# A hybrid decoder block: the short convolution's first gate joins the product stage, the state-space scan runs in three runs a block, the next head's jobs come first, the product stage's tiles are placed anew

## The chip, the core and the metric

The kernel runs on one core of a Trainium2 chip. Times are device microseconds (us) of that core. The engines are TensorE (PE in the profile; its weight loads are PEld), VectorE (DVE), ScalarE (ACT), GpSimd (POOL) and SyncE (SP, which here issues transfers).

## The reference

One layer over 16 meta tokens and 1024 tokens of width 1024. A normalised stream goes through one wide input projection, three mixers read parts of it, each mixer's output is projected, weighted by a sigmoid gate and merged, and one more projection follows.

```python
xn = rms_norm(x, norm_pre)
proj = xn @ w_in                                  # 1024 x 13856
(ssd_z, ssd_xbc, ssd_dt, sc_b, sc_c, sc_h, sc_g,
 dn_qkv, dn_z, dn_b, dn_a, gate_logits) = jnp.split(proj, ...)
y_ssd = ssd_mixer(...)     # conv, scan over chunks of 64, silu(z) gate, grouped rms_norm
y_sc  = short_conv_mixer(...)
y_dn  = gated_deltanet_mixer(...)   # 8 heads of 128: conv, l2 norm, delta rule, rms_norm, silu(z)
branch = jnp.einsum("btnw,nwd->btnd", jnp.stack([y_ssd, y_sc, y_dn], axis=2), w_branch)
merged = jnp.sum(jax.nn.sigmoid(gates) * branch, axis=2)
return x + rms_norm(merged @ w_out, norm_post)

def short_conv_mixer(b_gate, c_gate, h, gate, conv_w):
    y = b_gate * causal_depthwise_conv(c_gate * h, conv_w)
    return y * jax.nn.silu(gate)
```

The short convolution has four column blocks of the projection: c and h (before the convolution), the gate (`sc_g`) and b.

## The kernel before

Feature rows lie on the 128 partitions, tokens along the free axis. The normalised stream is held in the memory beside the engines as two parts, `xh` (the rounded value) and `xl` (the rest), tiles of 128 x 8 x 1040. A weight tile is split in the same way, and each product is three matmuls: xh by w high, xl by w high, xh by w low. They are called dense here; in the mixing stage lines 187 to 189 issue them, in the product stage lines 1144 to 1146.

**The mixing stage** (to 1217.8 us) is a list of jobs. A job is one block of 128 columns of the projection over all tokens: 8 k-tiles x 3 dense matmuls for each of three groups of 342 to 348 tokens, or of two groups of 512 where the meta tokens are not wanted. Each gated-delta head needs four jobs (`dn`+head+k, q, v, z). A tile t of the short convolution has three in this kernel, `sc`+t+c, h and g: `c * h`, its convolution on DVE, then the SiLU of g and the product, which goes to DRAM as `conv`. The state-space branch has jobs B and C for each of two groups, x and z for each of eight tiles.

The jobs fill slots, and each slot is woven with one mixer part: `dn_mix(h)` for the 8 heads (names `dm0` to `dm7`), `sd_mix(t)` for the 8 state-space tiles (`sm0` to `sm7`). The mixer is a generator, and each `yield` names a price that dense work should cover before the next piece of mixing; the table `GAPS` scales these by the kind of the slot. What is written out is the order on each engine, which runs its instructions in that order. Slot h of the heads holds the four jobs of head h+1 and some of the short convolution; the last state-space slot (kind `sl`) has three of the short convolution.

```python
    for h, n in enumerate((3, 3, 2, 3, 2, 3, 2, 3)):
        ...
        slot(4 + n, lambda h=h: beside(lambda: dn_mix(h, dnt[h]), early, 9), lambda n=n: sc_next(n), *fs)
```

The pieces that matter here: `dn_mix` turns k and v to token order (L508), multiplies k by q and k by k (L582, L587), solves the chunk's triangle in small 16-bit products, and runs the scan (L693 to L714: `ks`, `pn`, `su`, `o`); the norm of the head's output comes last (`ms`, L734 and L735). `sd_mix` does the same for the scan of the states (L852 to L876: `o`, `su`, the state `H`, `dg`) and sums squares for the grouped norm, whose reciprocal row (`sqa`, L901) goes to DRAM as `rin_d` (L902).

**The product stage** (from 1217.8 us) multiplies eight groups in a form with seven block products in place of eight (`py` and `pz` are its sums, each four quarters of 12 dense matmuls): the last gate of the short convolution (`cb`), for each branch its merging gate and its projection, and the output projection. The first product of a group whose input is the normalised stream reads `xh` and `xl` in place; other inputs are loaded (`tr`), then split on ACT (L1108) and DVE (L1109) into `th` and `tl`. Weights are split at L1124 and L1125. The state-space output is read back, scaled by `rin_d` (`scale_tasks`) and written out for its projection beside the first groups.

Of the kernel before, what the change touches and what calls it, by code (L numbers as in the profile page):

```python
# [1357 lines left out]
```

## Time and profile before

| | |
|---|---|
| Median of 3 runs | 1842.95 us (1842.75 to 1843.3) |
| Profiled execution, its own time | 1845.19 us |
| Its span, from the first to the last instruction | 1843.2 us |
| Mean granted TensorE clock | 0.996 |
| PE busy | 1806.2 us, 98% |
| DVE, ACT, POOL busy | 1302.7, 860.5, 220.3 us |
| Mixing stage, product stage | 0 to 1217.8, 1217.8 to 1843.2 us |

A busy matmul in the profile is shown with a duration that includes its pipeline, so two neighbours overlap; the spacing of work on PE is read from start to start. Instructions that the profile joins are counted by "x" at the row's end. The text in brackets behind a row is idle time of that engine just before it and what ended it.

### The profile page before, as it was taken

What the parts mean: (1) busy time and instruction counts of PE and PEld (TensorE: products, weight loads), DVE (VectorE), ACT (ScalarE), POOL (GpSimd) and SP (SyncE); (2) the same over time, 40 slices, a digit from 0 to 9 for tenths busy, and PEclk for the clock granted to TensorE, in tenths of its full rate; (3) what the DMA queues carried; (4) which work ended last, traced back from release to release, by engine and by line L of the source; (5) the groups of instructions that cost most, each with busy time, mean ns of one, the idle gap of its engine ahead of it and who ended that gap; (6) DMA issues with size and microseconds to landing.
All of it is one profiled execution on the core that took longest, in us unless ns stands there. A gap on an engine that the chain in (4) does not pass through costs nothing.

```text
span 1843.2 us, 27628 instructions
## 1 busy us (share of the span) xinstructions
PE 1806.2 (98%) x11067; PEld 1564.2 (85%) x11067; DVE 1302.7 (71%) x1898; ACT 860.5 (47%) x1373; POOL 220.3 (12%) x369
## 2 busy tenths in 40 slices
PE   6999999999999999999999999999999999999997
PEld 5988989888888889888989988978888888888886
DVE  6585766757576656757578867886686857967787
ACT  5443435353344425353445555445544455455454
POOL 3011111210112111110111101101000310000000
PEclk9999999999999999999999999999999999999999
DMA  5123262532224131202335323166566898763522
GB/s 156 49 70 104 75 172 61 132 87 90 59 64 114 47 81 39 65 26 62 75 90 175 84 77 104 35 222 228 175 218 230 295 289 222 209 192 133 194 98 92
DMA packets 149259, 229.96 MB, mean 125 GB/s; under 512 B 11393, under 2 KB 89406, under 8 KB 148458
## 3 DMA queue, kind: packets, MB, share of 16 engines
q1 hardware_dynamic: 129170, 166.31, 28.4%
q0 software_dynamic: 15344, 47.19, 10.6%
q10 hardware_dynamic: 4616, 14.69, 2.0%
q8 instruction: 87, 1.43, 0.3%
q14 instruction: 42, 0.34, 0.1%
HBM read 191.36 MB, written 68.27 MB: 141 GB/s over the span
## 4 chain that ended last, share of the span: by engine, by line
PE 85%; issue 4%; DVE 4%; DMA 3%; ACT 2%; POOL 1%; SPq 0%; DVEq 0%; ACTq 0%; POOLq 0%
PE py L1146 5%; PE py L1144 5%; PE py L1145 5%; PE pz L1145 4%; PE pz L1146 4%; PE pz L1144 4%; DMA ys<-y_sd 2%; DVE gt L1231 1%; DMA rin<-rin_d 0%; DMA gain<-in_norm_pre_dram 0%; DVE tl L1109 0%; DVE w L1125 0%; DMA raw<-in_w_in_dram 0%; PE sm L364 0%; PE dn7q L187 0%
## 5 line engine op out<-in xcount | busy, mean ns | idle before, releaser
L1146 PE MATMUL py<-th,w 128*128 128x512 f32 x496 | 193.2, 389 | 1.6 <-DVE w L1122 1.0
L1145 PE MATMUL py<-tl,w 128*128 128x512 f32 x496 | 193.0, 389 | 0.0
L1144 PE MATMUL py<-th,w 128*128 128x512 f32 x496 | 193.0, 389 | 0.0
L1109 DVE TENSOR_TENSOR tl<-tr,th 128x1024 fp32r<-128x1024 f32 x108 | 130.7, 1222 | 66.6 <-ACT th L1108 66.1
L1108 ACT CAST th<-tr 128x1024 fp32r<-128x1024 f32 x108 | 113.0, 1053 | 113.6 <-PE py L1146 53.6
L1144 PE MATMUL pz<-th,w 128*128 128x512 f32 x368 | 143.2, 389 | 0.0
L1145 PE MATMUL pz<-tl,w 128*128 128x512 f32 x368 | 143.2, 389 | 0.0
L1146 PE MATMUL pz<-th,w 128*128 128x512 f32 x368 | 143.2, 389 | 0.0
L1146 PEld LDWEIGHTS py<-th,w 128*128 128x128 f32 x496 | 93.1, 188 | 21.7 <-DVE w L1122 1.4
L1145 PEld LDWEIGHTS py<-tl,w 128*128 128x128 f32 x496 | 93.1, 188 | 19.4
L1144 PEld LDWEIGHTS py<-th,w 128*128 128x128 f32 x496 | 93.1, 188 | 19.3
L166 DVE TENSOR_TENSOR w<-raw,w 128x1024 fp32r<-128x1024 f32 x76 | 92.9, 1223 | 11.6 <-ACT w L165 11.3
L165 ACT CAST w<-raw 128x1024 fp32r<-128x1024 f32 x76 | 79.6, 1047 | 17.0 <-PE sc4h L189 8.3
L1145 PEld LDWEIGHTS pz<-tl,w 128*128 128x128 f32 x368 | 69.1, 188 | 14.4
L1144 PEld LDWEIGHTS pz<-th,w 128*128 128x128 f32 x368 | 69.1, 188 | 14.3
L1146 PEld LDWEIGHTS pz<-th,w 128*128 128x128 f32 x368 | 69.1, 188 | 14.3
L1156 ACT COPY u<-py 128x1024 f32<-128x1024 f32 x34 | 34.5, 1015 | 56.2 <-PE py L1146 56.2
L1169 DVE TENSOR_TENSOR u<-pz,u 128x1024 f32<-128x1024 f32 x34 | 41.3, 1218 | 4.2 <-PE pz L1146 4.2
L1265 POOL COPY tick<-th 128x1 f32<-128x1 f32 x12 | 14.7, 1228 | 120.5 <-ACT th L1108 120.5
L1175 ACT ACTIVATE gt<-u 128x1024 f32<-128x1024 f32 x14 | 14.8, 1059 | 28.9 <-DVE u L1169 25.7
L479 ACT ACT_TABLE_LOAD x20 | 25.7, 1283 | 4.8 <-PE sd2z L189 1.4
L500 ACT ACT_TABLE_LOAD x19 | 24.4, 1283 | 0.3
(1858 smaller groups left out, 5446.8 us busy)
## 6 DMA issues: line engine op xcount, KB each, us to landing
raw<-in_w_in_dram SPq DMA_DIRECT2D x76, 512.0 KB, 4.2
tr<-x_t SPq DMA_DIRECT2D x32, 512.0 KB, 4.2
tr<-x SPq DMA_DIRECT2D x14, 512.0 KB, 6.3
ys<-y_sd POOLq DMA_DIRECT2D x16, 256.0 KB, 7.3
tr<-dn_t SPq DMA_DIRECT2D x8, 512.0 KB, 6.2
gt<-conv SPq DMA_DIRECT2D x4, 1024.0 KB
tr<-sc_t SPq DMA_DIRECT2D x8, 512.0 KB, 3.8
tr<-sd_t SPq DMA_DIRECT2D x8, 512.0 KB, 3.8
```

Source lines behind the costliest of these rows:

```text
L165: A.copy(wh, raws[i])
L166: V.tensor_tensor(wl, raws[i], wh.bitcast(F32), ALU.subtract)
L479: lambda o, c0, n: A.activation(dst[:, c0 - META:c0 - META + n], o, fn), name=name)
L500: A.activation(f, f, AF.Exp)
L1108: A.copy(h, src)
L1109: V.tensor_tensor(l, src, h.bitcast(F32), SUB)
L1144: PE.matmul(o, lhsT=w[:, 0, k, cs], rhs=r1, start=fresh and k == 0, stop=False, skip_group_check=not fresh)
L1145: PE.matmul(o, lhsT=w[:, 0, k, cs], rhs=r2, start=False, stop=False, skip_group_check=not fresh)
L1146: PE.matmul(o, lhsT=w[:, 1, k, cs], rhs=r1, start=False, stop=k == HK - 1, skip_group_check=not fresh)
L1156: A.copy(t, g.ps["y", u])
L1169: V.tensor_tensor(k, t, k, ADD)
L1231: V.scalar_tensor_tensor(o, o, tot, fin["x", t][:, es], ALU.mult, ADD)
```

## The change

- The short convolution's tile has two jobs, c and h. The convolution itself goes to DRAM, and its gate `sc_g` becomes a further group of the product stage (`POST = ("cg", "cb")`). The slots of the heads hold 2, 2, 2, 2, 2, 2, 1, 1 short convolution jobs in place of 3, 3, 2, 3, 2, 3, 2, 3, and the last slot two in place of three.
- In a head's slot the next head's four jobs now come ahead of the short convolution's.
- k and q of a head lie in one tile, and k by k and k by q are one product of 256 columns.
- `sd_mix` issues a block's sums (`su`), then its chain of states on DVE, then the products with the states (`o`), where before they alternated chunk by chunk.
- `xh` and `xl` start on a multiple of 256 bytes with rows of 1088 values, the first true token at such a multiple too; before, rows had 1040 values.
- In the product stage, tiles of the rings `tr`, `th` and `rin` and the first blocks are allocated ahead in a fixed order, the first weight's load and splitting are put at high priority, the scaling of the state-space output is closed one step later and starts a step earlier, and two small tiles share a ring.
- The last pause of a head, ahead of its norm (`ms`), has a price of 4500 in place of 2400.

```diff
@@ -21,6 +21,7 @@
+XO, XW = 48, 1088
...
@@ -145,8 +146,7 @@
-    xh = xp.tile([P, KT, TK], F32R, name="xh")
-    xl = xp.tile([P, KT, TK], F32R, name="xl")
+    xh, xl = (xp.tile([P, KT, XW], F32R, name=n, align_bytes=256)[:, :, XO:XO + TK] for n in ("xh", "xl"))
...
@@ -512,11 +512,11 @@
-            tiles["k"] = big(n + "k", "kT", 2)
+            kq = tiles["kq"] = pool.tile([P, 2, TK], F32, name=n + "kq", tag="kq", bufs=2)
+            tiles["k"], tiles["q"] = kq[:, 0, :], kq[:, 1, META:]
-            tiles["q"] = big(n + "q", "qT", 2)
...
@@ -576,19 +577,23 @@
+            an = sq_mat(b, n + "An", "An", 2)
             if b is not B0:
-                pkq = mt(f"{n}kq{b.i}")
-                for j in range(b.n):
-                    PE.matmul(pkq[:b.l, b.col(j)], lhsT=kT[:, b.tok(j)], rhs=qT[:, b.out(j)], start=True, stop=True)
                 PT[b] = sq_mat(b, n + "PT", "PT", 2)
-                V.tensor_tensor(PT[b], b.split(pkq[:b.l, :b.w]), f, ALU.mult)
-            pkk = mt(f"{n}kk{b.i}")
             for j in range(b.n):
-                PE.matmul(pkk[:b.l, b.col(j)], lhsT=kT[:, b.tok(j)], rhs=kT[:, b.tok(j)], start=True, stop=True)
-            an = sq_mat(b, n + "An", "An", 2)
-            for j in range(b.n):
-                V.scalar_tensor_tensor(an[:, j, :], pkk[:b.l, b.col(j)], nbeta[:b.l, b.c0 + j, h:h + 1], f[:, j, :],
-                                       ALU.mult, ALU.mult)
+                if j % 2 == 0:
+                    pkk = mt(f"{n}kk{b.i}{j}")[:b.l, :4 * b.l].rearrange("p (c a l) -> p c a l", c=2, a=2)
+                if b is B0:
+                    PE.matmul(pkk[:, 0, 0, :], lhsT=kT[:, b.tok(j)], rhs=kT[:, b.tok(j)], start=True, stop=True)
+                else:
+                    PE.matmul(pkk[:, j % 2], lhsT=kT[:, b.tok(j)], rhs=kq[:, :, b.tok(j)], start=True, stop=True)
+                if j % 2 and b is not B0:
+                    V.tensor_tensor(PT[b][:, j - 1:j + 1, :], pkk[:, :, 1, :], f[:, j - 1:j + 1, :], ALU.mult)
+                if j % 2 or b is B0:
+                    for jj in range(j // 2 * 2, j + 1):
+                        V.scalar_tensor_tensor(an[:, jj, :], pkk[:, jj % 2, 0, :], nbeta[:b.l, b.c0 + jj, h:h + 1],
+                                               f[:, jj, :], ALU.mult, ALU.mult)
...
@@ -728,7 +733,7 @@
-        yield 2400
+        yield 4500
...
@@ -759,15 +764,17 @@
-
-        def g(w):
-            gs = tmp(n + "g")
-            yield from act_job(gs, n + "g")(w)
-            V.tensor_tensor(tl["a"], tl["a"], gs[:, :SEQ], ALU.mult)
             for j in range(2):
-                (GP if t == KT - 1 else DMA).dma_start(conv[t // HK, j][:, t % HK, :], tl["a"][:, j * HALF:(j + 1) * HALF])
-
-        return (C_CC + t * P, c), (C_CH + t * P, hh), (C_CG + t * P, g)
+                (GP if t == KT - 1 else DMA).dma_start(conv[t // HK, j][:, t % HK, :], acc[:, j * HALF:(j + 1) * HALF])
+
+        return (C_CC + t * P, c), (C_CH + t * P, hh)
+
...
@@ -834,13 +841,32 @@
+
+        H = {b: pool.tile([P, b.n, P], F32, name=f"{n}H{b.i}", tag="XU128", bufs=2) for b in BIG}
             px = to_tm(xT, b, n + "px")
-            yield 800
+            yield 800 if b is B0 else 1600
+            psu = mt(f"{n}su{b.i}")
+            for j in range(b.n):
+                c = b.c0 + j
+                if c == NCH - 1:
+                    continue
+                PE.matmul(psu[:, j * P:(j + 1) * P], lhsT=Btm[:b.l, c, :], rhs=xw[:b.l, c, :], start=True, stop=True)
+            for j in range(b.n):
+                c = b.c0 + j
+                if c == NCH - 1:
+                    continue
+                Hn = H[B1][:, 0, :] if b is B0 else H[b][:, j + 1, :] if j + 1 < b.n else H[B2][:, 0, :]
+                if b is B0:
+                    V.tensor_copy(Hn, psu[:, :P])
+                else:
+                    for a in range(2):
+                        sl = slice(a * 64, (a + 1) * 64)
+                        V.scalar_tensor_tensor(Hn[:, sl], H[b][:, j, sl], etot[:, c, h0 + a:h0 + a + 1],
+                                               psu[:, j * P + a * 64:j * P + (a + 1) * 64], ALU.mult, ALU.add)
...
@@ -848,25 +874,10 @@
-                    yield 1875
+                    yield 2600
                 po = psm.tile([P, 512], F32, tag="o", name=f"{n}o{b.i}", bufs=1)
-            for j in range(b.n):
-                c = b.c0 + j
-                if H is not None:
-                    PE.matmul(po[:, b.col(j)], lhsT=H, rhs=CT[:, b.out(j)], start=True, stop=True)
-                if c < NCH - 1:
-                    psu = mt(f"{n}su{c}")
-                    PE.matmul(psu[:, :P], lhsT=Btm[:b.l, c, :], rhs=xw[:b.l, c, :], start=True, stop=True)
-                    Hn = pool.tile([P, P], F32, name=f"{n}H{c}", tag="S", bufs=2)
-                    if H is None:
-                        V.tensor_copy(Hn, psu[:, :P])
-                    else:
-                        for a in range(2):
-                            sl = slice(a * 64, (a + 1) * 64)
-                            V.scalar_tensor_tensor(Hn[:, sl], H[:, sl], etot[:, c, h0 + a:h0 + a + 1], psu[:, sl],
-                                                   ALU.mult, ALU.add)
-                    H = Hn
-                yield 600
+                for j in range(b.n):
+                    PE.matmul(po[:, b.col(j)], lhsT=H[b][:, j, :], rhs=CT[:, b.out(j)], start=True, stop=True)
...
@@ -979,10 +990,10 @@
-    for h, n in enumerate((3, 3, 2, 3, 2, 3, 2, 3)):
+    for h, n in enumerate((2, 2, 2, 2, 2, 2, 1, 1)):
         fs = [lambda h=h: dn_jobs(h + 1, dnt[h + 1])] if h < DN_H - 1 else [
             lambda: sdg_jobs(0, grps[0]), lambda: sd_jobs(0, sdt[0])]
-        slot(4 + n, lambda h=h: beside(lambda: dn_mix(h, dnt[h]), early, 9), lambda n=n: sc_next(n), *fs)
+        slot(4 + n, lambda h=h: beside(lambda: dn_mix(h, dnt[h]), early, 9), *fs, lambda n=n: sc_next(n))
...
@@ -991,7 +1002,7 @@
-        fs.append((lambda t=t: sd_jobs(t + 1, sdt[t + 1])) if t < KT - 1 else lambda: sc_next(3))
+        fs.append((lambda t=t: sd_jobs(t + 1, sdt[t + 1])) if t < KT - 1 else lambda: sc_next(2))
...
@@ -1037,6 +1048,15 @@
+    spare = {}
+
+    def ring(tag, shape, dt, bufs=4):
+
+        spare[tag] = [c1.tile(list(shape), dt, name=f"{tag}_{n}", tag=tag, bufs=bufs) for n in range(bufs)]
+
+    def take_tile(tag, shape, dt, name, bufs=4):
+        return spare[tag].pop(0) if spare.get(tag) else c1.tile(list(shape), dt, name=name, tag=tag, bufs=bufs)
...
@@ -1065,10 +1085,11 @@
-                    t = self.blk[tag] = block(tag)
-                    self.wsrc(t, j, i)
-
-    POST = ("cb",)
+                    if self.n or tag not in self.blk:
+                        self.blk[tag] = block(tag)
+                    self.wsrc(self.blk[tag], j, i)
+
+    POST = ("cg", "cb")
...
@@ -1233,23 +1254,33 @@
+        todo = []
+
+        def close():
+            i, j, u, t, r = todo.pop(0)
+            n = i * HK + 2 * u
+            for k in range(2):
+                w = (snw if i == j else nsnw)[:, n + k:n + k + 1]
+                V.scalar_tensor_tensor(t[:, k, :], t[:, k, :], w, r, ALU.mult, ALU.mult)
+            for dst in quarters("sd", i, j):
+                background(GP, dst[:, 2 * u:2 * u + 2, :], t)
                 for u in range(2):
+                    if todo:
+                        close()
+                    if u == 0:
...
@@ -1267,13 +1298,21 @@
+
-    g0.load("a11")
-    for u in range(2):
-        t_prep(g0, 0, u)
-        w_prep(g0, 0, u)
+    with tc.high_priority(offset=400):
+        g0.load("a11")
+    for tag in ("a22", "a12", "a21"):
+        g0.blk[tag] = block(tag)
+    ring("tr", (P, 2, HALF), F32)
+    ring("rin", (P, HALF), F32, 1)
-    g0.load("a12", "a21", "a22")
+    ring("th", (P, 2, HALF), F32R)
+    with tc.high_priority(offset=400):
+        for u in range(2):
+            t_prep(g0, 0, u)
+            w_prep(g0, 0, u)
+    g0.load("a12", "a22", "a21")
```

On DVE at the border between the two stages, before: `sc7c` and `sc7a` are the last short convolution tile, `sqa` and `sm7sl` belong to the norm row of the state-space branch, `w_00` and `w_01` are the low parts of the first product weights.

```order
L756 TENSOR_TENSOR sc7c<-sc7h_12844,sc7c 128x342
L759 TENSOR_SCALAR sc7a<-sc7c,cols 128x1024
L889 TENSOR_TENSOR sqa_2_11766<-sqa_2_11766,sm7sq_12868 128x512
L761 SCALAR_TENSOR_TENSOR sc7a<-sc7c,cols,sc7a 128x1024
L897 TENSOR_TENSOR sm7sl_12902<-sqa_1_11765,sm7sh_12900 128x512
L761 SCALAR_TENSOR_TENSOR sc7a<-sc7c,cols,sc7a 128x1024
L897 TENSOR_TENSOR sm7sl_12912<-sqa_2_11766,sm7sh_12910 128x512
L901 RECIPROCAL sqa_1_11765<-sqa_1_11765 1x512
L901 RECIPROCAL sqa_2_11766<-sqa_2_11766 1x512
L766 TENSOR_TENSOR sc7a<-sc7a,sc7g 128x1024
L1125 TENSOR_TENSOR w_00_12984<-a__12982,w_00_12984 128x1024
```

The same place after the change:

```order
L891 TENSOR_TENSOR sd7z<-pair_9853,sd7z 128x512
L761 TENSOR_TENSOR sc7c<-sc7h_12294,sc7c 128x342
L764 TENSOR_SCALAR sc7a<-sc7c,cols 128x1024
L900 TENSOR_TENSOR sqa_2_11245<-sqa_2_11245,sm7sq_12291 128x512
L908 TENSOR_TENSOR sm7sl_12323<-sqa_1_11244,sm7sh_12321 128x512
L766 SCALAR_TENSOR_TENSOR sc7a<-sc7c,cols,sc7a 128x1024
L908 TENSOR_TENSOR sm7sl_12333<-sqa_2_11245,sm7sh_12331 128x512
L766 SCALAR_TENSOR_TENSOR sc7a<-sc7c,cols,sc7a 128x1024
L912 RECIPROCAL sqa_1_11244<-sqa_1_11244 1x512
L912 RECIPROCAL sqa_2_11245<-sqa_2_11245 1x512
L1146 TENSOR_TENSOR w_00_12373<-a__12358,w_00_12373 128x1024
```

The product with the gate (L766 of before) is gone; the two reciprocals (L901, now L912) still stand directly ahead of the first weight's low part.

On PE at the same border, before: `ms` are the products of the norm row, `sc7g` the last gate job, of whose second group of 512 tokens the last row here is the first of 24 matmuls.

```order
L189 MATMUL sc7g_12895<-xh,w_12805 128x512
L187 MATMUL sc7g_12895<-xh,w_12805 128x512
L899 MATMUL sm7ms_12909<-sm7sl_12912,cmeanr 128x512
L188 MATMUL sc7g_12895<-xl,w_12805 128x512
L189 MATMUL sc7g_12895<-xh,w_12805 128x512
L187 MATMUL sc7g_12941<-xh,w_12805 128x512
```

After the change:

```order
L187 MATMUL sc7h_12294<-xh,w_12113 128x342
L188 MATMUL sc7h_12294<-xl,w_12113 128x342
L189 MATMUL sc7h_12294<-xh,w_12113 128x342
L909 MATMUL sm7ms_12320<-sm7sh_12321,cmeanr 128x512
L910 MATMUL sm7ms_12320<-sm7sl_12323,cmeanr 128x512
L909 MATMUL sm7ms_12330<-sm7sh_12331,cmeanr 128x512
L910 MATMUL sm7ms_12330<-sm7sl_12333,cmeanr 128x512
L1165 MATMUL py<-xh,w_00_12373 128x512
L1166 MATMUL py<-xl,w_00_12373 128x512
L1167 MATMUL py<-xh,w_00_12373 128x512
```

Behind the last product of the norm stood the 24 matmuls of the second group and a few more; now the first product of the product stage (`py`) follows it directly, with the rest of the short convolution's `sc7h` ahead.

On PE at the border between heads 4 and 5, before: `dm5pv` turns the values of head 5, `dm5pb` a later step of it.

```order
L189 MATMUL sc4g_6973<-xh,w_6890 128x512
L187 MATMUL sc4g_6973<-xh,w_6890 128x512
L508 MATMUL dm5pv_6867<-ident,dn5v 16x128
L508 MATMUL dm5pv_6881<-ident,dn5v 128x128 x4
L508 MATMUL dm5pv_6901<-ident,dn5v 128x128 x4
L565 MATMUL dm5pb_6917<-ident,dm5ktm 128x16
```

After the change:

```order
L188 MATMUL sc4h_6583<-xl,w_6389 128x342
L189 MATMUL sc4h_6583<-xh,w_6389 128x342
L739 MATMUL dm4ms_6621<-dm4oh_6574,cmeanr 128x512
L740 MATMUL dm4ms_6621<-dm4ol_6576,cmeanr 128x512
L508 MATMUL dm5pk_6636<-ident,dn5kq 16x128
L187 MATMUL dn6k_6642<-xh,w_6548 128x348
L188 MATMUL dn6k_6642<-xl,w_6548 128x348
```

Before, four short products of head 5 in a row followed the gate's first matmuls; now the norm of head 4 ends late beside `sc4h`, the keys of head 5 (`dm5pk`) are turned first, and the jobs of head 6 (`dn6k`) lead its slot.

## Rows read from the trace of the kernel before

**Rows 1.** Page, section 1: engine, busy us (share of the span) x instructions.

```profile
PE 1806.2 (98%) x11067; PEld 1564.2 (85%) x11067; DVE 1302.7 (71%) x1898; ACT 860.5 (47%) x1373; POOL 220.3 (12%) x369
```

**Rows 2.** Busy time by stretch: the heads, and the product stage.

```profile
87.70:931.20 843.50, 837.58 (x6147) 741.04 (x6145) 568.11 (x986) 363.02 (x756) 126.99 (x217) 1.00 0.29 80
1217.80:1843.20 625.40, 612.50 (x2688) 505.36 (x2688) 458.70 (x431) 306.65 (x333) 44.71 (x62) 0.99 0.62 198
```

**Rows 3.** Waits of PE: us in total, times, longest.

```profile
PE py L1144 <- ACT w L1124: 1.6, 1, 1.6
...
PE py L1146 <- DVE w L1122: 1.0, 1, 1.0
PE dm3pv L508 <- ACT dn3v L470: 0.8, 1, 0.8
...
PE sc4g L187 <- DVE sc4c L756: 0.7, 1, 0.7
PE dm0ms L735 <- POOL dm0ol L727: 0.7, 1, 0.7
...
PE dm6su L705 <- ACT dm6vn L700: 0.5, 1, 0.5
```

**Rows 4.** Timeline of PE: start, us, engine, line, operation.

```profile
1211.15 0.39 PE L187 MATMUL sc7g<-xh,w 128*128 128x512 f32 x1
...
1215.33 0.40 PE L187 MATMUL sc7g<-xh,w 128*128 128x512 f32 x1
```

**Rows 5.** Timeline of PE in the product stage.

```profile
1231.61 0.39 PE L1144 MATMUL pz<-xh,w 128*128 128x512 f32 x1
...
1242.73 0.39 PE L1144 MATMUL py<-th,w 128*128 128x512 f32 x1
...
1264.51 0.39 PE L1144 MATMUL pz<-th,w 128*128 128x512 f32 x1
```

**Rows 6.** Timeline of PE, groups of 342.

```profile
1202.07 0.32 PE L188 MATMUL sc7h<-xl,w 128*128 128x342 f32 x1
...
1203.02 0.32 PE L188 MATMUL sc7h<-xl,w 128*128 128x342 f32 x1
```

**Rows 7.** Timeline of all engines at the border between the stages.

```profile
1199.37 1.09 PE L876 MATMUL sm7dg<-sm7F,sm7xd 128*64 128x128 f32 x16
...
1203.80 0.40 PE L187 MATMUL sc7g<-xh,w 128*128 128x512 f32 x1
...
1209.41 6.55 DVE L901 RECIPROCAL sqa<-sqa 1x512 f32<-1x512 f32 x2
...
1216.22 0.24 ACTq L902 DMA_DIRECT2D rin_d<-sqa  x1
1216.71 1.99 ACT L1124 CAST w<-a__12982 128x1024 fp32r<-128x1024 f32 x2
...
1217.80 0.50 PE L1144 MATMUL py<-xh,w 128*128 128x512 f32 x1 [1.62 <-ACT w L1124]
...
1219.26 0.73 PE L1146 MATMUL py<-xh,w 128*128 128x512 f32 x1 [0.73 <-DVE w L1125]
...
1222.78 0.40 PE L1145 MATMUL py<-xl,w 128*128 128x512 f32 x1
```

**Rows 8.** Timeline of PE: products of 128 and of 216 columns.

```profile
74.81 0.53 PE L418 MATMUL pcum<-smda,tri 128*128 128x216 f32 x2
75.17 0.53 PE L420 MATMUL ptot<-smda,cmean 128*128 128x216 f32 x2
...
106.70 1.05 PE L582 MATMUL dm0kq<-dn0q,dn0k 128*128 128x128 f32 x8
107.60 1.06 PE L587 MATMUL dm0kk<-dn0k 128*128 128x128 f32 x8
```

**Rows 9.** Timeline of PE: one step of head 4's scan.

```profile
595.25 0.39 PE L698 MATMUL dm4pn<-dm4R,dm4Y 128*128 128x128 f32 x2
...
596.17 0.47 PE L705 MATMUL dm4su<-dm4vn,dm4kd 128*128 128x128 f32 x2
```

More of the change, by code (lines that the diff above doesn't have):

```diff
@@ L536, in dn_mix @@
         qT, kT, vT, zT = (tiles[c] for c in "qkvz")
+        kq = tiles["kq"]
         n = f"dm{h}"
@@ L718, in dn_mix @@
                 continue
-            osq = pool.tile([P, HALF], F32, name=f"{n}osq{b.i}", tag="osq", bufs=2)
+            osq = pool.tile([P, HALF], F32, name=f"{n}osq{b.i}", tag="An128", bufs=2)
             A.activation(osq, po, AF.Square)
@@ L761, in hh, with pair @@
                 V.scalar_tensor_tensor(acc, ch[:, h0 + k:h0 + k + SEQ], sc_cw(k, t), acc, ALU.mult, ALU.add)
-        def g(w):
-            gs = tmp(n + "g")
-            yield from act_job(gs, n + "g")(w)
-            V.tensor_tensor(tl["a"], tl["a"], gs[:, :SEQ], ALU.mult)
             for j in range(2):
-                (GP if t == KT - 1 else DMA).dma_start(conv[t // HK, j][:, t % HK, :], tl["a"][:, j * HALF:(j + 1) * HALF])
-        return (C_CC + t * P, c), (C_CH + t * P, hh), (C_CG + t * P, g)
+                (GP if t == KT - 1 else DMA).dma_start(conv[t // HK, j][:, t % HK, :], acc[:, j * HALF:(j + 1) * HALF])
+        return (C_CC + t * P, c), (C_CH + t * P, hh)
+    pairs = {}
+    def pair(i):
+        if i not in pairs:
+            pairs[i] = pool.tile([P, 2, TK], F32, name=f"pair{i}", tag="kq", bufs=2)
+        return pairs[i]
     def sdg_jobs(g, grp):
@@ L779, in cj @@
         def cj(w):
-            grp["C"] = big(n + "C", "kT", 2)
+            grp["C"] = pair(g)[:, 0, :]
             yield from conv_job(lambda i: sd_cw(i, 10 + g), grp["C"], META, n + "C", sd_cb(10 + g))(w)
@@ L789, in xj @@
         def xj(w):
-            tiles["x"] = big(n + "x", "qT", 2)
+            tiles["x"] = pair(t % 2)[:, 1, :]
             yield from conv_job(lambda i: sd_cw(i, t), tiles["x"], 0, n + "x", sd_cb(t))(w)
@@ L835, in heads @@
             return ap.rearrange("p c (a b) -> p c a b", a=2)
-        H = None
+        H = {b: pool.tile([P, b.n, P], F32, name=f"{n}H{b.i}", tag="XU128", bufs=2) for b in BIG}
         for b in BLOCKS:
@@ L1096, in t_load @@
         for u in range(2):
-            t = g.raw[ph, u] = c1.tile([P, 2, HALF], F32, name=f"tr{g.n}_{ph}{u}", tag="tr", bufs=4)
+            t = g.raw[ph, u] = take_tile("tr", (P, 2, HALF), F32, f"tr{g.n}_{ph}{u}")
             DMA.dma_start(t, g.ops[OPS[ph]][:, 2 * u:2 * u + 2, :])
@@ L1104, in t_prep @@
             return
-        h = c1.tile([P, 2, HALF], F32R, name=f"th{g.n}_{ph}{u}", tag="th", bufs=4)
+        h = take_tile("th", (P, 2, HALF), F32R, f"th{g.n}_{ph}{u}")
         l = c1.tile([P, 2, HALF], F32R, name=f"tl{g.n}_{ph}{u}", tag="tl", bufs=4)
@@ L1205, in out_setup @@
         fin["ss"] = c1.tile([P, SEQ // P, 4], F32, name="oss", tag="oss")
-        fin["junk"] = c1.tile([P, HALF], F32, name="ojunk", tag="ojunk")
+        fin["junk"] = c1.tile([P, HALF], F32, name="ojunk", tag="rin")
     def residual(tag, t0):
@@ L1238, in scale_tasks @@
                 js = slice(j * HALF, (j + 1) * HALF)
-                r = c1.tile([P, HALF], F32, name=f"rin{i}{j}", tag="rin")
-                DMA.dma_start(r, rin_d[i][:, js].broadcast_to([P, HALF]))
                 for u in range(2):
+                    if todo:
+                        close()
+                    if u == 0:
+                        r = take_tile("rin", (P, HALF), F32, f"rin{i}{j}", 1)
+                        DMA.dma_start(r, rin_d[i][:, js].broadcast_to([P, HALF]))
                     t = c1.tile([P, 2, HALF], F32, name=f"ys{i}{j}{u}", tag="gpost", bufs=2)
-                    n = i * HK + 2 * u
                     for k in range(2):
-                        background(GP, t[:, k, :], y_sd[n + k][:, js])
+                        background(GP, t[:, k, :], y_sd[i * HK + 2 * u + k][:, js])
+                    todo.append((i, j, u, t, r))
                     yield 0
-                    for k in range(2):
-                        w = (snw if i == j else nsnw)[:, n + k:n + k + 1]
-                        V.scalar_tensor_tensor(t[:, k, :], t[:, k, :], w, r, ALU.mult, ALU.mult)
-                    for dst in quarters("sd", i, j):
-                        background(GP, dst[:, 2 * u:2 * u + 2, :], t)
                     yield 0
+        close()
     scale, sd_sums, sc_sums = scale_tasks(), sums("sd"), sums("sc")
@@ L1258, in extra @@
     def extra(n, q):
-        if q == 2 and 9 <= n < 25:
+        if q == 2 and 8 <= n < 25:
             next(scale, None)
```

## The prediction

> **What bounds the kernel now.** First the page: TensorE (PE) is busy 98% of the span [rows 1]. That number can hide idle issue slots, so the next view is the one by stretch [rows 2]: in the head stage (87.7 to 931.2 us) PE is busy for 837.58 of 843.50 us, in the product stage for 612.50 of 625.40, while VectorE (DVE) has a third and a quarter of its time free. Then the waits of PE alone [rows 3]: after the opening 88 us the largest single wait is 1.6 us, at the border between the stages, and the next are 1.0, 0.8, 0.7 and 0.7. So PE issues nearly without a break, and the time is the number of its matmuls by their spacing. An edit pays by taking away matmuls or spacing, and costs where dense matmuls no longer cover a chain of other engines.
>
> The spacing comes from the timeline, as start to start. A dense matmul of 512 columns: 18 of them from 1211.15 to 1215.33, 0.2322 us each [rows 4]. In the product stage with xh and xl as the moving operand: 48 in 11.12 us, 0.2317; with its own tiles th and tl: 96 in 21.78 us, 0.2269 [rows 5]. A dense matmul of 342 columns: six in 0.95 us, 0.158 [rows 6].
>
> **The gate moved to the product stage.** Eight dense gate jobs go, each 2 column groups x 8 k-tiles x 3 = 48 matmuls: 384 x 0.2322 = 89.2 us. A group of the product stage comes in: 7 products x 4 quarters x 12 = 336 matmuls x 0.2269 = 76.2 us. Net -13.0 us. The group's preparation and the gate's SiLU lie on DVE and ScalarE (ACT), free for a quarter and a half of that stage [rows 2], so I cost them at nothing; without that cover the SiLU would come on top, 8 pieces as large as one of the two weight casts that take 1.99 us together [rows 7].
>
> **What the last gate job covered.** In the before kernel this job was the cover of the last mixing chain. The last diagonal products of the scan end at 1200.46 [rows 7]; from there the chain runs through DVE, ACT and PE to the two reciprocals of the norm row (6.55 us on DVE from 1209.41), the rin_d transfer in ACT's queue (1216.22), the cast of the first product weight (1216.71) and its low part on DVE. PE starts the product stage at 1217.80 and waits once more, until 1219.26. Beside this stand 3.4 us of the sc7h job (to 1203.80) and the whole sc7g job. The order of the changed kernel keeps the chain: on DVE both reciprocals still stand ahead of the low part of the weight, on ACT the rin_d transfers ahead of the cast. But PE has only 27 dense matmuls of 342 columns (27 x 0.158 = 4.3 us) and four of the norm (0.9 us) behind the last diagonal product. Chain: 1219.26 - 1200.46 = 18.8 us, plus 0.9 because DVE waits for the last sc7h group in the middle of it, less 0.5 for the gate's SiLU on ACT that is gone: 19.2 us. PE work beside it: 4.3 + 0.9 + 0.45 for the first two products = 5.65. Lost: 13.5 us. Before, the same stretch lost 1.62 + 0.73 and some 0.1. So the border costs **+11.2 us** more; 11.2 / 13.0 of the gate's gain goes there. The clock: after the wait of before, nine matmuls take 3.52 us instead of 2.1, the 1.2 GHz level [rows 7]; the longer wait brings this too, and I take it as equal.
>
> **Alignment of xh and xl.** Every k-row now starts at the same place of a 256-byte line, and the 512-column groups start on one. The rows show two spacings for 512 columns, 0.2322 and 0.2269, and the slower belongs to xh and xl [rows 4, 5]. I take the faster: 16 z jobs x 48 = 768 x 0.0053 = -4.1 us, and -0.5 us for the 96 first products. The other 52 dense jobs (3744 matmuls) use groups of 342 to 348 columns that still start off a line; nothing shows them aligned. Bounds: the same 2.3% of 0.158 gives -13.5 us; none gives 0, and 1 ns worse +3.7 us. I take -3, near none, since their starts stay uneven.
>
> **k and q beside each other.** 64 pairs of 128-column products become 64 products of 256. Four of 128 take 0.90 us, 0.448 a pair; one of 216 columns takes 0.36, which by its columns makes 0.43 for 256 [rows 8]. 64 x 0.02 = -1.3 us. These run at the streaming rate already, so I give nothing for fewer instructions.
>
> **The state scan in three runs.** The same 64 + 64 + 128 products in other places; in a run each costs 0.22 us [rows 8]. Turns between such runs and dense work fall from 450 to 412. No row prices a turn; a pass of 0.11 either way bounds it at 4 us to either side, and I take 0. The chain of states, eight short DVE instructions, moves off PE's path: by the order over 5 us of dense work stand between the sums and their use.
>
> **The next head's jobs lead.** At a head's border PE waits for the v job's SiLU (0.8), for DVE at the next job (0.7) and for the tail on GpSimd (0.7) [rows 3]. Now the head's inputs are done a job or more earlier, and the tail has 5.9 us instead of about 4 between its last product and its second norm matmul. I take -3.5 us. What queues behind: the store of the convolution now sits in SP's queue behind DVE's convolution rather than the gate's product; raw weights behind it are a job ahead, so nobody waits.
>
> **Fewer dense matmuls between dependent steps.** Eight head slots have 6, 6, 6, 6, 6, 6, 5, 5 jobs, before 7, 7, 6, 7, 6, 7, 6, 7. From one scan product to the next that needs it the chain wants 0.92 us (595.25 to 596.17) [rows 9]. Counted in the order, 7 of 8 such steps of head 6 and 3 of head 7 have less, mostly 0.70; before two each. With the solver's steps, now 0.6 to 0.8 us apart where most had 1.0 to 2.3, I put 0.5 us a slot on six slots and 1.5 on the last two: +6 us, bounded by 0 and 15 (0.05 us on each of some 290 steps).
>
> **Product stage.** Of the waits for DVE there, 1.0 [rows 3] stems from the scaling of the state-space output, which now is closed a step later; DVE's order still holds it among the first weights. -0.5, bounds -1.6 and +4.
>
> **Sum.** -13.0 + 11.2 - 4.6 - 3 - 1.3 - 3.5 + 6 - 0.5 = -8.7 us. The profiled execution took 1845.19 us with a span of 1843.2; the timed runs have their median at 1842.95, so the profile stands 2.2 us above them and I subtract from the median: **1834.2 us**.
>
> **Rivals.** (1) The border is covered after all: the chain is cut shorter or PE's last matmuls fall later. For it: the first weight's load is put first and its tiles no longer lie on late ones. Against: the order of DVE and ACT. It gives 1834.2 - 11.2 = 1823. (2) Aligned rows go below 0.2269: the start of a row, not the stream, makes the gap. For it: 512 columns at 2.4 GHz are 0.2133, below both spacings; against: th and tl do not go below 0.2269. At 0.2157 the z jobs alone give another 768 x 0.0112 = 8.6 us: 1825.6. The Trainium skill, "TensorE: Matmul & The Clock Gate", section "Back-to-back issue gap", states just this: N/2.4 + 2.5 ns, 215.7 ns for 512 columns; the trace differs by 11 ns at best [rows 5] and by 16 ns in dense jobs [rows 4]. (3) Slower: the woven slots starve. In the slots of 5 and 6 jobs each dependent step arrives late and, DVE being in order, delays the next. Its price is some 290 steps by the mean added wait; from 0.065 us above my own 0.02 it outweighs everything else, and at 0.07 the time is 1834.2 + 14.5 = 1848.7. For it: distances as short as the chain. Against: the 6-job heads of before, where in the scan no wait passes 0.5 us [rows 3]. (4) No change: alignment gives nothing and the border costs 14: 1834.2 + 7.6 + 2.8 = 1844.6.
>
> **Chances.** The forecast 0.52, its own range 1825 to 1840; border covered 0.10; faster rows 0.08; no change 0.16; starved 0.14. A measurement of this kernel tells 0.2% (3.7 us) from no change, so faster (below 1839.3) is 0.69, the same 0.16, slower 0.15. The range for 8 in 10: 1820 to 1846.
>
> **What would show it.** Right: PE idle for 11 to 14 us just ahead of its first product, with the reciprocals inside, then the 1.2 GHz level; 512-column dense spacing near 0.227; waits of 0.1 to 0.3 us in heads 6 and 7; no PE wait for a v job. Wrong: a border wait under 6 us, or spacing of the 342-column jobs changed by more than 2 ns, which would move more than any other term.

## The result, and the profile after

The changed kernel takes 1859.34 us (median of 4 runs, 1857.99 to 1861.48), the kernel before 1843.12 beside it: a ratio of 1.0089, 95% interval 1.0077 to 1.0102. It is 16 us slower where 9 us faster was forecast, outside the range. The profiled execution took 1858.86 us with a span of 1857.2, 14.0 above that of before.

The page, engines over the span, answers to [rows 1]:

```profile
PE 1804.5 (97%) x10891; PEld 1557.2 (84%) x10891; DVE 1339.5 (72%) x1946; ACT 871.1 (47%) x1378; POOL 217.6 (12%) x369
```

PE works as long as before with 176 matmul records fewer, and its share fell by a point: the lost time is in waits and in slow matmuls. The busy time by stretch says where (columns as in [rows 2]): heads 0 to 5, heads 6 and 7, state-space tiles 0 to 6, tile 7 with the border, product stage:

```profile
86.50:676.00 589.50, 586.99 (x4371) 523.37 (x4369) 415.59 (x746) 252.15 (x547) 93.87 (x171) 1.00 0.32 88
676.00:863.80 187.80, 184.61 (x1366) 159.11 (x1365) 136.06 (x240) 82.09 (x180) 28.79 (x46) 1.00 0.19 54
863.80:1099.40 235.60, 235.57 (x1500) 209.89 (x1498) 191.15 (x336) 125.16 (x169) 35.63 (x33) 1.00 0.38 105
1099.40:1142.80 43.40, 31.79 (x222) 29.59 (x220) 30.51 (x49) 15.49 (x23) 4.21 (x7) 0.89 0.41 140
1142.80:1857.20 714.40, 693.23 (x3024) 570.50 (x3024) 515.90 (x478) 351.28 (x378) 40.27 (x58) 0.99 0.59 189
```

The same stretches of before, from its trace, and the prediction's terms, each put on the stretch where it acts:

| stretch | before, us | after, us | difference | forecast |
|---|---|---|---|---|
| up to head 0's mixing | 87.6 | 86.5 | -1.1 | -0.4 |
| heads | 850.6 | 777.3 | -73.3 | -81.0 |
| state-space tiles 0 to 6 | 235.1 | 235.6 | +0.5 | -2.3 |
| tile 7 and border | 44.5 | 43.4 | -1.1 | -0.1 |
| product stage | 625.4 | 714.4 | +89.0 | +75.2 |
| sum | | | +14.0 | -8.7 |

So 13.8 us of the miss lie in the product stage, 7.7 in the heads, 2.8 in the state-space tiles. The border came nearly as forecast. The opening differs from run to run by more than it does here: over the runs below it takes 85.6 to 88.9 us. The waits of PE (us in total, times, longest) in place of [rows 3]:

```profile
PE py L1165 <- ACT w L1145: 8.2, 1, 8.2
PE pz L1165 <- ACT pz L1174: 4.8, 1, 4.8
PE sm7ms L910 <- DVE sm7sl L908: 3.4, 2, 2.4
PE py L1167 <- DVE w L1146: 3.3, 2, 3.0
...
PE pz L1167 <- DVE w L1146: 1.2, 1, 1.2
...
PE py L1167 <- DVE w L1143: 0.8, 1, 0.8
```

The first and the third are the border, 11.6 us together. The other four are new, 10.1 us together, and they come after the product stage has begun.

**The border**, all engines, answers to [rows 7]:

```profile
1123.91 1.09 PE L887 MATMUL sm7dg<-sm7F,sm7xd 128*64 128x128 f32 x16
...
1133.84 0.80 PE L910 MATMUL sm7ms<-sm7sl,cmeanr 128*128 128x512 f32 x1 [1.07 <-DVE sm7sl L908]
...
1134.89 6.54 DVE L912 RECIPROCAL sqa<-sqa 1x512 f32<-1x512 f32 x2
...
1138.26 3.46 ACTq L913 DMA_DIRECT2D rin_d<-sqa  x2
1141.76 1.99 ACT L1145 CAST w<-a__12358 128x1024 fp32r<-128x1024 f32 x2 [6.40 <-DVE sqa L912]
...
1142.85 0.80 PE L1165 MATMUL py<-xh,w 128*128 128x512 f32 x1 [8.22 <-ACT w L1145]
...
1144.11 0.80 PE L1167 MATMUL py<-xh,w 128*128 128x512 f32 x1
```

From the end of the last diagonal products (1125.00) to the third product of the product stage (1144.11) are 19.1 us, forecast 19.2. The same instructions stand in it, in the order shown ahead.

**The new waits.** The scalings of the state-space output (`ys`) on VectorE, before and after; the first and the last time are those of their first and last start:

```profile
L1249 DVE SCALAR_TENSOR_TENSOR ys<-ys,snw,rin x8: 741/746/752, 1244.2 to 1480.4; 128x512 f32<-128x512 f32 x8
```

```profile
L1264 DVE SCALAR_TENSOR_TENSOR ys<-ys,snw,rin x8: 744/748/752, 1172.3 to 1253.3; 128x512 f32<-128x512 f32 x8
```

VectorE between 1229 and 1242 us, in the second group of the product stage:

```profile
1229.26 0.75 DVE L1264 SCALAR_TENSOR_TENSOR ys<-ys,nsnw,rin 128x512 f32<-128x512 f32 x1 [3.89 <-DMA ys<-y_sd]
...
1231.14 0.75 DVE L1264 SCALAR_TENSOR_TENSOR ys<-ys,nsnw,rin 128x512 f32<-128x512 f32 x1
1231.81 1.22 DVE L1190 TENSOR_TENSOR u<-pz,u 128x1024 f32<-128x1024 f32 x1
1232.94 1.22 DVE L1146 TENSOR_TENSOR w<-a__12667,w 128x1024 fp32r<-128x1024 f32 x1
...
1238.58 0.75 DVE L1264 SCALAR_TENSOR_TENSOR ys<-ys,snw,rin 128x512 f32<-128x512 f32 x1 [3.17 <-DMA ys<-y_sd]
```

GpSimd, which issues the loads of `ys`, and PE in the same window:

```profile
1222.26 0.54 POOL L127 DMA_DIRECT2D sd_n<-ys  x1 [10.43 <-DVE ys L1264]
1222.80 1.08 POOL L127 DMA_DIRECT2D ys<-y_sd  x2
1232.19 0.54 POOL L127 DMA_DIRECT2D sd_n<-ys  x1 [8.31 <-DVE ys L1264]
1232.72 1.08 POOL L127 DMA_DIRECT2D ys<-y_sd  x2
```

```profile
1234.21 0.50 PE L1167 MATMUL py<-th,w 128*128 128x512 f32 x1 [3.03 <-DVE w L1146]
...
1245.93 0.76 PE L1165 MATMUL pz<-th,w 128*128 128x512 f32 x1 [4.80 <-ACT pz L1174]
...
1249.45 0.40 PE L1167 MATMUL pz<-th,w 128*128 128x512 f32 x1
```

It is one chain that goes round. A load of the state-space output is issued behind the store of the one before (1222.80 behind 1222.26) and lands some 6 us later. Its scaling (L1264) stands in DVE's order ahead of the weight's low part (L1146), so DVE stops for 3.89 us, the weight comes at 1234.16, and PE waits 3.03. The scaling lets GpSimd store and issue the next load (1232.72), at which DVE stops again, and the copy that PE needs (L1174) stands on ACT behind work that waits for that DVE. The clock adds to it: after the wait of 4.80 eight matmuls take 3.52 us (1245.93 to 1249.45), 0.44 each, at a granted clock of 0.53 of full speed, so nearly all of them at the 1.2 GHz level; at 0.2267 they would take 1.8. Eight more run at 0.42 from 1235.71, 1.5 us behind the wait of 3.03.

**The spacing** of dense 512-column matmuls in the mixing stage, to be read beside [rows 4]: 22 from 999.83 to 1004.82, 0.2268 us.

```profile
999.83 0.39 PE L189 MATMUL sd4z<-xh,w 128*128 128x512 f32 x1
...
1004.82 0.39 PE L187 MATMUL sd4z<-xh,w 128*128 128x512 f32 x1
```

**The heads.** The first product of heads 5, 6, 7 and of the state-space branch:

```profile
578.29 0.27 PE L508 MATMUL dm5pk<-ident,dn5kq 128*16 128x128 f32 x1
...
675.96 0.27 PE L508 MATMUL dm6pk<-ident,dn6kq 128*16 128x128 f32 x1
...
767.71 0.27 PE L508 MATMUL dm7pk<-ident,dn7kq 128*16 128x128 f32 x1
...
863.80 0.27 PE L508 MATMUL sm0px<-ident,pair 128*16 128x128 f32 x1
```

Head 5 has 6 jobs and takes 97.7 us, head 6 has 5 and takes 91.7: a job of 72 dense matmuls less (72 x 0.158 = 11.4 us) saves 6.0. The other 5.4 are lost between its steps. Head 7, also with 5, takes 96.1 us (before, with 7 jobs, 116.0).

### The profile page after: what moved, and what is told of

Read it like the earlier page. It is cut to its first block, busy times and chain, and to the rows that moved or that the text cites. A ratio compares the mean times of both kernels' runs of the same rounds, so it can differ in the third digit from the quotient of the medians.

```text
span 1857.2 us, 27382 instructions
## 1 busy us (share of the span) xinstructions
PE 1804.5 (97%) x10891; PEld 1557.2 (84%) x10891; DVE 1339.5 (72%) x1946; ACT 871.1 (47%) x1378; POOL 217.6 (12%) x369
## 4 chain that ended last, share of the span: by engine, by line
PE 85%; issue 7%; DVE 3%; DMA 2%; ACT 1%; POOL 1%; SPq 0%; DVEq 0%; ACTq 0%; POOLq 0%
PE py L1167 6%; PE py L1166 6%; PE py L1165 6%; PE pz L1165 5%; PE pz L1166 5%; PE pz L1167 5%; DMA ys<-y_sd 1%; DMA a__12667<-in_w_branch_dram 1%; DVE gt L1252 1%; DMA gain<-in_norm_pre_dram 0%; DMA raw<-in_w_in_dram 0%; PE dn3v L187 0%; PE dn1v L187 0%; PE dn6v L187 0%; PE dn5v L187 0%
## 5 line engine op out<-in xcount | busy, mean ns | idle before, releaser
L1167 PE MATMUL py<-th,w 128*128 128x512 f32 x560 | 218.9, 391 | 4.1 <-DVE w L1146 3.3
L1165 PE MATMUL py<-th,w 128*128 128x512 f32 x560 | 218.6, 390 | 0.0
L1166 PE MATMUL py<-tl,w 128*128 128x512 f32 x560 | 218.4, 390 | 0.0
L1130 DVE TENSOR_TENSOR tl<-tr,th 128x1024 fp32r<-128x1024 f32 x122 | 148.2, 1222 | 86.2 <-ACT th L1129 85.3
L1129 ACT CAST th<-tr 128x1024 fp32r<-128x1024 f32 x122 | 127.7, 1053 | 124.9 <-PE py L1167 60.1
L1165 PE MATMUL pz<-th,w 128*128 128x512 f32 x416 | 162.7, 391 | 4.8 <-ACT pz L1174 4.8
L1167 PE MATMUL pz<-th,w 128*128 128x512 f32 x416 | 162.4, 391 | 1.2 <-DVE w L1146 1.2
L1166 PE MATMUL pz<-tl,w 128*128 128x512 f32 x416 | 162.5, 391 | 0.0
L1167 PEld LDWEIGHTS py<-th,w 128*128 128x128 f32 x560 | 105.4, 188 | 27.3 <-DVE w L1146 4.1
L1166 PEld LDWEIGHTS py<-tl,w 128*128 128x128 f32 x560 | 105.5, 188 | 22.1
L1165 PEld LDWEIGHTS py<-th,w 128*128 128x128 f32 x560 | 105.5, 188 | 21.9
L1165 PEld LDWEIGHTS pz<-th,w 128*128 128x128 f32 x416 | 78.4, 189 | 21.6 <-ACT pz L1174 5.2
L1167 PEld LDWEIGHTS pz<-th,w 128*128 128x128 f32 x416 | 78.5, 189 | 18.0 <-DVE w L1146 1.6
L1174 ACT COPY pz<-py 128x1024 f32<-128x1024 f32 x16 | 16.0, 998 | 22.5 <-PE py L1167 22.5
```

The source lines that it names most:

```text
L1129: A.copy(h, src)
L1130: V.tensor_tensor(l, src, h.bitcast(F32), SUB)
L1165: PE.matmul(o, lhsT=w[:, 0, k, cs], rhs=r1, start=fresh and k == 0, stop=False, skip_group_check=not fresh)
L1166: PE.matmul(o, lhsT=w[:, 0, k, cs], rhs=r2, start=False, stop=False, skip_group_check=not fresh)
L1167: PE.matmul(o, lhsT=w[:, 1, k, cs], rhs=r1, start=False, stop=k == HK - 1, skip_group_check=not fresh)
L1174: A.copy(g.ps["z", u], g.ps["y", u])
```

## The experiments

Theory A: the gate's move brings the losses, by three ways that are separate: the uncovered border, slots too short for the head's chain, and the scalings of the state-space output in a burst behind slow loads. The rivals stand with each. Times are medians; ratios are to the kernel before on the same chip. Going by these intervals, two versions can be told apart from some 3 to 4 us on.

**The gate's move alone.** The kernel before, with

```diff
...
-        return (C_CC + t * P, c), (C_CH + t * P, hh), (C_CG + t * P, g)
+        return (C_CC + t * P, c), (C_CH + t * P, hh)
...
-    for h, n in enumerate((3, 3, 2, 3, 2, 3, 2, 3)):
+    for h, n in enumerate((2, 2, 2, 2, 2, 2, 1, 1)):
...
-    POST = ("cb",)
+    POST = ("cg", "cb")
```

> The kernel before with only the gate's move: its 8 jobs gone, the slots at 2,2,2,2,2,2,1,1 and 2, the group cg in the product stage. Theory A (the move itself brings the losses: the uncovered border, two starved head slots, and a burst of the state-space scaling in the product stage's second group): 1843 - 13 + 11 + 8 + 10 = 1859 us, PE waits of 8 us or more behind the border. Rival B (the burst comes from the new closing of the scaling and the new places of the tiles): waits behind the border below 2 us and 1843 - 13 + 11 + 8 = 1849 us. Rival C (the new order of jobs and the scan in runs starve the heads, not the slots' length): heads 6 and 7 lose nothing, 1851 us.

Measured 1877.22 us, ratio 1.0182 (1.0166 to 1.0197): 18 slower than the whole change, and as much above theory A's sum. The waits behind the border are there:

```profile
PE pz L1140 <- ACT pz L1149: 4.8, 1, 4.8
...
PE py L1142 <- DVE w L1121: 1.9, 1, 1.9
PE py L1142 <- DVE w L1118: 1.6, 1, 1.6
```

So the burst needs neither the new closing nor the new places (rival B falls as far as the move goes). The heads take 798.9 us, 21.6 more than in the changed kernel: rival C falls the other way round, and the rest of the change wins back there what short slots cost.

**The gate back.** The changed kernel with the gate's move reversed.

> The changed kernel with the gate back in the mixing stage (slots 3,3,2,3,2,3,2,3 and 3, no group cg), all else as changed. Theory A: what is left is worth the alignment's 3 us and some 2 to 4 of the new job order: 1836 to 1839 us, PE waits behind the border below 2 us. Rival B (closing and places bring the burst): the waits of about 10 us stay, 1846 to 1849 us.

Measured 1844.13 us, ratio 1.0006 (0.9996 to 1.0015). Theory A was 5 to 8 too low: waits of 5.3 us for DVE stayed in the product stage (2.9, 1.2, 1.2), where before had 1.0 [rows 3]. Neither theory had this: with the gate in its old place the rest of the change brings waits of its own, and which part of it does was not tried. They go where the scalings are spread too (the last runs). The heads gained 2.9 us against before (847.7 and 850.6).

**The scalings spread.** The changed kernel with

```diff
-                V.scalar_tensor_tensor(t[:, k, :], t[:, k, :], w, r, ALU.mult, ALU.mult)
+                sc = V.scalar_tensor_tensor(t[:, k, :], t[:, k, :], w, r, ALU.mult, ALU.mult)
+                if k == 0:
+                    tc.keep_in_program_order(sc)
```

which puts each scaling on DVE behind what the program's text has ahead of it.

> The changed kernel with each scaling of the state-space output pinned on VectorE behind what the program text has ahead of it, so that the eight scalings are spread over 16 steps and not issued in a burst. Theory A: the waits of PE behind the border (9.8 us) fall below 2 and the time to about 1850 us. Rival D (these waits come from transfers that share the queues, whatever DVE's order is): they stay above 7 us and the time within 2 us of 1859.

Measured 1845.54 us, ratio 1.0013 (1.0003 to 1.0022), 13.8 below the changed kernel. No wait of PE is left behind the border; these are all from 1130 us on, and the stage takes 699.7 us:

```profile
PE py L1165 <- ACT w L1145: 8.2, 1, 8.2
PE sm7ms L910 <- DVE sm7sl L908: 3.4, 2, 2.4
```

```profile
1146.10:1845.80 699.70, 688.76 (x3024) 568.74 (x3024) 515.27 (x478) 352.11 (x377) 41.19 (x58) 0.99 0.60 193
```

The same bytes move, on a share of 0.60 of the DMA engines instead of 0.59. It is DVE's order that made the transfers dear (rival D falls). The time fell 4 us further than expected. By this row and the one of the changed kernel above, the product stage is 14.7 us shorter: 10.2 us of PE's idle time went, and 4.5 us of its busy time for the same 3024 matmuls, most of it the two runs of eight slow matmuls behind the waits (3.3 us).

**The old closing.** The changed kernel with `scale_tasks` and its start as before.

> The changed kernel with the scaling of the state-space output as before (closed in its own step, begun a step later). Theory A (the burst comes with the gate's group, which takes the step after the first two groups, not with the closing): waits of 8 to 13 us behind the border and 1857 to 1862 us. Rival B (the new closing makes the burst): waits below 3 us, 1847 to 1850.

Measured 1860.14 us, ratio 1.0087 (1.0070 to 1.0104), with waits of 4.9, 3.6 and 0.8 there: as the changed kernel. With the gate moved, closing a step later changes nothing.

**The border's reciprocals.** The changed kernel with

```diff
-                A.activation(sqa[b], ps, AF.Sqrt, bias=eps, scale=P / 512)
-                V.reciprocal(sqa[b][0:1, :], sqa[b][0:1, :])
+                for v in range(4):
+                    vs = slice(v * 32, (v + 1) * 32)
+                    A.activation(sqa[b][vs, :P], ps[vs, v * P:(v + 1) * P], AF.Sqrt, bias=eps[vs, :], scale=P / 512)
+                V.reciprocal(sqa[b][:, :P], sqa[b][:, :P])
...
```

> The changed kernel with the norm row's reciprocals taken over four groups of partitions at once: [128x128] in place of [1x512], twice, so some 1.6 us of DVE in place of 6.5 at the border. Theory A (the border's wait is the chain through the reciprocals): the wait of 8.2 us falls to 3 to 4 and the time by about 5, to 1854. Rival E (it is the transfer of rin_d on ACT's queue, or the weight's load, that ends last): the wait stays above 6 us, time 1857 to 1859.

Measured 1856.47 us, ratio 1.0070 (1.0055 to 1.0085), 2.9 below the changed kernel, at the limit of what the runs can tell, where 5 were expected. At the border:

```profile
1136.14 0.94 DVE L914 RECIPROCAL sqa<-sqa 128x128 f32<-128x128 f32 x1
...
1139.11 1.99 ACT L1147 CAST w<-a__12370 128x1024 fp32r<-128x1024 f32 x2 [1.54 <-DVE sqa L914]
...
1140.21 0.80 PE L1167 MATMUL py<-xh,w 128*128 128x512 f32 x1 [4.33 <-ACT w L1147]
```

The reciprocals went from 6.54 to 1.9 us and the wait from 8.2 to 4.3. The chain runs through them; ACT's roots, now in four pieces each, take a part of the gain (2.96 us in place of 1.38).

**The short slots elsewhere.** The changed kernel with

```diff
-    for h, n in enumerate((2, 2, 2, 2, 2, 2, 1, 1)):
+    for h, n in enumerate((2, 2, 2, 1, 1, 2, 2, 2)):
```

> The changed kernel with the short slots moved: the heads' slots have 2,2,2,1,1,2,2,2 short convolution jobs in place of 2,2,2,2,2,2,1,1, so heads 3 and 4 weave beside 5 jobs and heads 6 and 7 beside 6. Theory A (a slot of 5 jobs starves the chain of dependent steps): the losses of 4 to 5 us a head move from heads 6 and 7 to heads 3 and 4, time unchanged within 3 us. Rival F (heads 6 and 7 lose by what else lies there, the jobs and tiles of the state-space branch): they keep their loss, and the time is the same or higher.

Measured 1863.38 us, ratio 1.0111 (1.0096 to 1.0126). The first products of heads 3 to 6:

```profile
384.70 0.27 PE L508 MATMUL dm3pk<-ident,dn3kq 128*16 128x128 f32 x1
...
476.51 0.27 PE L508 MATMUL dm4pk<-ident,dn4kq 128*16 128x128 f32 x1
...
567.31 0.27 PE L508 MATMUL dm5pk<-ident,dn5kq 128*16 128x128 f32 x1
...
665.00 0.27 PE L508 MATMUL dm6pk<-ident,dn6kq 128*16 128x128 f32 x1
```

Heads 3 and 4, now with 5 jobs, take 91.8 and 90.8; head 6 with 6 takes 97.7, as head 5. The loss goes with the 5 jobs (rival F falls for head 6). Head 7 takes 105.3 with 6 jobs: there the job is worth 9.2 of its 11.4 us, so its loss with 5 was only 2.2. The time rose by 4 us, a little over the 3 allowed: two slots in the middle cost somewhat more than these two at the end.

**The old order of jobs.** The changed kernel with the short convolution's jobs ahead of the next head's.

```diff
-..., *fs, lambda n=n: sc_next(n))
+..., lambda n=n: sc_next(n), *fs)
```

> The changed kernel with the old order of jobs in a slot: the short convolution's first, then the next head's. With the gate moved alone the head stage lost 23 us, in the changed kernel 5 to 7. Theory A (the next head's jobs in front is what takes most of that back): the head stage loses 10 to 16 us more, time 1869 to 1875. Rival G (the joined products, the pause of 4500 or the scan in runs take it back): within 3 us of 1859.

Measured 1880.83 us, ratio 1.0207 (1.0190 to 1.0224), 21.5 above the changed kernel, more than expected. The heads take 797.2 us (777.3): 20 us hang on what comes first in a slot, and rival G falls. Two thirds of them lie in heads 1 and 7 (105.3 and 101.9 us, against 97.8 and 96.1); in head 1 PE waits once for 3.6 us on the scan's state. Head 6, the other one with 5 jobs, loses nothing (91.0 against 91.7).

**The alignment undone.** The changed kernel with

```diff
-    xh, xl = (xp.tile([P, KT, XW], F32R, name=n, align_bytes=256)[:, :, XO:XO + TK] for n in ("xh", "xl"))
+    xh, xl = (xp.tile([P, KT, TK], F32R, name=n) for n in ("xh", "xl"))
```

> The changed kernel with xh and xl placed as before (rows of 1040 values, no start at 256 bytes). If the alignment brings what the spacings say (0.2329 us for 512 columns in the mixing stage of before, 0.2290 after, groups of 342 to 348 unchanged), it is worth 768 x 0.0039 = 3 us, and this kernel takes about 1862. Rival: the groups of 342 to 348 gain too, 6 us or more; or nothing is gained and the time stays at 1859.

Measured 1864.56 us, ratio 1.0113 (1.0097 to 1.0129): the time is 5 us longer (4.5 by the spans). Spacing: 0.2327 us for 512 columns off a line of 256 bytes, 0.2290 as a mean over those on one; groups of 342 to 348 columns the same within 1 ns. That makes 3 us. By stretch the two traces agree with it: the heads differ by 0.5 us (777.8 and 777.3), the state-space tiles by 1.9 (237.5 and 235.6), border and product stage by 0.1. The other 2.0 lie in the opening (88.5 and 86.5), which differs as much among kernels with aligned rows. So the alignment is worth some 2.5 to 3 us. It came in the state-space z jobs (median 0.233 to 0.227); in the heads' z jobs, which the mixer's products break into short runs, the median only went from 0.234 to 0.232.

**Versions with both fixes.** Three kernels with the scalings pinned and the reciprocals over four groups: the changed kernel (with the norm's tail at high priority too), the one with the gate back, and the kernel before.

> The changed kernel with the scalings pinned, the reciprocals over four groups of partitions, and the norm's tail at high priority. If the burst (13.8 us measured) and the border's reciprocals (2.9 measured) are separate losses, they add: 1859 - 13.8 - 2.9 = 1842.5, and 1 to 2 less by the priority: 1841 to 1842.5. Rival: with the burst gone the shorter border only moves the wait into the product stage: 1845.

> The version with the gate back in the mixing stage (1844.1), with the scalings pinned and the reciprocals over four groups. It still had 6 us of waits of PE for VectorE in the product stage (2.9, 1.2, 1.2, 0.7) by the same burst, and 2.3 at the border. Theory A: the waits of the product stage go, some 4 to 6 us, and 1 to 2 at the border: 1838 to 1839, below both kernels. Rival: the product stage's waits there have another source: 1843 to 1844.

> The kernel before with two edits of the experiments alone: the scalings pinned, the reciprocals over four groups of partitions. If these two edits are what made the version with the gate back fast, this one comes near it, 1838 to 1840; the rest of the change (alignment, joined products, runs, job order) is then worth 1 to 3 us with the gate in its old place. Rival: the before kernel has no burst to lose, 1842 to 1843.

Measured 1844.27 us (ratio 1.0006, 0.9997 to 1.0016), 1837.26 (0.9966, 0.9955 to 0.9978) and 1842.29 (0.9993, 0.9983 to 1.0002). The version with the gate back is below both kernels. Its waits of PE from 1130 us on are

```profile
PE py L1171 <- ACT w L1151: 1.8, 1, 1.8
PE py L1173 <- DVE w L1152: 0.6, 1, 0.6
```

Two expectations missed. On the changed kernel the shorter border added 1.3 us to the spread scalings, which the runs can't tell from nothing, and not 2.9; a new wait of 1.5 for ACT's copy stands in its product stage, and at the border the high priority put waits of 3.1 and 2.2 where 3.4 was. And the two fixes alone do little for the kernel before, so the 5 us between it and the best version are the rest of the change: alignment, joined products, runs, job order and places together pay once the burst is out of the way. Between the first two versions the gate's place is all but the only difference: its move costs 7 us here even without the burst.

## Why the prediction was wrong

**The step that failed** is the one on the product stage: "Of the waits for DVE there, 1.0 stems from the scaling ... DVE's order still holds it among the first weights. -0.5, bounds -1.6 and +4." It measured +13.8 us with its clock; spreading the scalings on DVE took that back whole. I saw that DVE's order holds the scalings among the weights, and took the wait of before for their price. But in the trace of before GpSimd's queue held them back: four loads, and then the fifth only behind stores of the last gate's group, over 130 us later:

```profile
1266.91 1.10 POOL L126 DMA_DIRECT2D ys<-y_sd  x2
1392.61 0.54 POOL L1184 DMA_DIRECT2D sc<-gt  x1 [124.59 <-DVE gt L1182]
1393.14 1.06 POOL L126 DMA_DIRECT2D sd_t<-ys  x2
1398.91 0.53 POOL L1184 DMA_DIRECT2D sc<-gt  x1 [4.71 <-DVE gt L1182]
1399.44 1.11 POOL L126 DMA_DIRECT2D ys<-y_sd  x2
```

With a group more ahead of these stores, all eight scalings follow each other from 1172 to 1253 us (before: 1244 to 1480). That the store is what held them is read from the orders; it was not tried by itself. The runs fit it on both sides: with the gate's move alone seven loads come in a row and the eighth waits behind that store (1425.86), and with the gate back the fifth load again stands behind a wait of 124.6 us (1393.03). It would have been seen ahead of the run by setting the eight instructions in DVE's order beside the 7 us that a load of `ys` takes to land.

**Fewer dense matmuls between dependent steps.** The direction was right and the sizes were wrong on both sides. I put 0.5 us on each of six slots with 6 jobs and 1.5 on two with 5. The 6-job heads lost nothing (head 5: 97.7 us; head 4 of before, also with 6 jobs, 97.9), head 6 lost 5.4 and head 7 some 2. The waits in head 6 are 0.2 to 0.9 us, where 0.1 to 0.3 were named as the sign. The mechanism of the third rival holds, for slots of 5 jobs and not as a mean price on all.

**The next head's jobs lead.** Forecast -3.5, from the waits of [rows 3]. With the gate in its old place the heads as a whole gained 2.9. With the gate moved the order is worth 20 us, which no row of before could show, for it had no such slots in this order. Both terms of the heads together were +2.5; the stretch came 7.7 above its forecast. An estimate from the runs: 3.7 of it are the alignment (forecast -4.2 by the jobs that lie there, measured -0.5), 1.6 the slots (+7.6 in place of +6) and 2.4 the order (-1.1, what is left of the 2.9 without alignment and joined products).

**The gate and the border.** Net -13.0 for the dense work stands: PE's matmuls fell and rose as counted, and with the scalings spread the product stage takes 74.3 us more than before, forecast 75.2. The border's 11.2 measured 10.0 (the stretch of tile 7 lost one gate job of 11.1 us and shrank by 1.1).

**Alignment.** 512 columns moved to 0.2268 us, as forecast (0.2269), in the state-space jobs, hardly in the heads, and the other groups not at all. So of the 7.6 us some 2.5 to 3 came. Rival 2 had the spacing go on to 0.2157: it did not. The Trainium skill, "TensorE: Matmul & The Clock Gate", section "Back-to-back issue gap", gives N/2.4 + 2.5 ns for an isolated matmul, 215.8 ns for 512 columns; the trace lies 11 ns above that with aligned rows too, and it decides.

**The state scan in three runs.** Forecast 0. The state-space tiles took 235.6 us, and 237.5 without the alignment, where before took 235.1. So the runs may have cost 1 to 2 us there; they were not tried by themselves.

**Rivals 1 and 4.** The border was not covered (8.2 us of wait, and 3.4 ahead of it). "No change" had the border and the alignment right or nearly so, but not the burst.

**Two numbers of the working.** The clock behind the wait of before is eight matmuls in 3.52 us, not nine [rows 7], so 1.9 us at the 2.4 GHz level and not 2.1. And by its own 290 steps the third rival wipes out the gain of 8.7 us from 0.03 us above my 0.02, not from 0.065. Neither moved the sum.

## What to carry to other kernels

When an edit moves a stage's work, look at the background transfers whose place nobody wrote down: an engine that works in order stops at the first instruction whose load has not landed, and everything behind it waits. Set each such instruction's place in the order against the load's measured time to land. And cover is not a mean: the slots of 6 jobs lost nothing here and one of 5 lost 5.4 us, so price the shortest slots by themselves.
